# One Strassen level for the widening MLP product, its weight sums on VectorE

## The chip, the cores and the metric

The kernel runs on one core of one Trainium2 chip. The metric is the device time of one launch in microseconds (us). TensorE (PE in the profile) multiplies; VectorE (DVE), ScalarE (ACT) and GpSimd (POOL) do the rest; SyncE (SP) issues most DMAs. L203 and the like are lines of the kernel before; lines of the changed kernel are higher by 46 in its helpers.

## The reference

One step of a two-layer decoder trunk for 512 prompt rows and 64 sample rows, which share the weights; the kernel keeps them as 576 columns (NT) of one activation matrix with 1024 rows (D_MODEL), in float32. Per layer: a norm, the input product, attention and pooling branches, gates, the product with w_o, and then the part that is changed:

```python
h2 = rmsnorm(x, norm2)
x = x + jnp.square(jax.nn.relu(h2 @ w_up)) @ w_down
```

`w_up` is 1024 x 4096 (the widening product), `w_down` 4096 x 1024 (the narrowing one). Outputs are the two activations after a last norm, and the updated caches and pool states.

## The kernel before

**Two-part operands.** Every product runs in float32r. A weight tile (128 x 1024, 512 KB) is fetched into `raw`, copied by ACT to a high part `wh` (`wsplit`), and DVE subtracts to get a low part `wl` (`settle`). Activations are split likewise (`split`). A product of one 128-row weight block with an activation block is three passes: high by high, high by low, low by high. Each pass covers 576 columns as two matmuls of 256 and 320 columns (`HALF`), so that they fall into two PSUM banks; `gemm8` (through `gemm`, L228) runs eight blocks of 128 rows, 48 matmuls, into one PSUM buffer `mm`, of which there are two.

**The MLP.** Layers run one after the other, and in each the product with w_o ends in eight tiles `xs[f]` (the residual) and eight split tiles `h2`, already scaled by the gains of the second norm; the norm's own factor `rb` is applied later. The widening product has 32 tiles of 128 rows, the narrowing product eight. They alternate in four chunks: eight widening tiles, then the eight narrowing tiles of the chunk before, each of which adds the contribution of eight widening tiles to `xs[f]`. For a widening tile, `relu2` takes the PSUM buffer by one DVE instruction (`z`, ReLU and factor), squares it on ACT (`zz`) and splits it. For a narrowing tile DVE adds the buffer to `xs[f]` (`xr<-xr,mm`). In layer 0 the last chunk also squares and splits for the next layer (`hn`); in layer 1 `last` runs it in column ranges of 320 and 256 and `finish` does the last norm.

**What sets the order.** The program is written out by hand: engines run their own instructions in the order in which the Python code emits them. `wnext()` hands out the next weight tile and, while doing so, emits the fetch of tiles up to five places ahead and the split of tiles up to three places ahead; `wh` and `wl` have three buffers each. `side(...)` and `tick(...)` place side work by a planned clock. `move` emits a one-element DVE copy (`beat`) that paces cache copies on POOL's DMA queue. All helpers record their DVE, ACT and POOL instructions under one line (L203), so the rows below are told apart by the names of the tiles.

Of the kernel before, what the change touches and what calls it, by code (L numbers as in the profile page):

```python
# [7 lines left out]
F32 = mybir.dt.float32  # L8
# [23 lines left out]
NCONST = _n  # L32

UNITS = ("d", "a", "b", "e", "c")


@with_exitstack
def hybrid_decoder_kernel(ctx: ExitStack, tc: tile.TileContext, a, o):
# [36 lines left out]
    def g2(l, k):  # L75
        return gains[:, 16 + 8 * l + k:16 + 8 * l + k + 1]
# [10 lines left out]
    for l in range(L):  # L87
        for p in range(2):
            for u, unit in enumerate(UNITS):
                if unit == "e" and p == 1:  # L90
                    continue
                seq += [(a["wq"][l, p, u, i], 1024) for i in range(2)]
        seq += [(a["wu"][l, g], 1024) for g in (3, 2, 1, 0)]
        for wg, wp_, m, lead in (("wgb", "wpb", 512, LEADB), ("wga", "wpa", 256, LEADA)):
            for f in range(8):
                seq += [(a[wg][l, i], 1024) for i in range(lead[f - 1] if f else 0, lead[f])]
                seq.append((a[wp_][l, f], m))
        seq += [(a["wo"][l, f], 1024) for f in range(8)]
        for c in range(5):
            if c < 4:  # L100
                seq += [(a["wup"][l, 8 * c + f], 1024) for f in range(8)]
            if c:
                seq += [(a["wd"][l, c - 1, f], 1024) for f in range(8)]
    raws, cut, owed, spare = [], [], [], []
    pos = [0, 0, 0]

    def wfetch(n):
        while pos[0] < min(n, len(seq)):
            src, w = seq[pos[0]]
            raw = wp.tile([128, 1024], F32, tag="raw", name="raw", bufs=2)  # L110
            Q.dma_start(raw[:, :w], src)
            raws.append((raw, w))
            pos[0] += 1

    def wsplit(n):
        while pos[1] < min(n, len(seq)):
            raw, w = raws[pos[1]]
            if pos[1] < len(seq) - 5:
# [5 lines left out]
            owed.append((lo[:, :w], raw[:, :w], hi[:, :w].bitcast(F32)))  # L124
            cut.append((hi, lo))
            pos[1] += 1

    def settle():
        while owed:
            V.tensor_sub(*owed.pop(0))  # L130

    def wnext():
        i = pos[2]
        pos[2] += 1
        wfetch(i + 2)
        for n in range(1, 4):
            settle()
            wsplit(i + n)
            if n < 3:
                settle()  # L140
                wfetch(i + 2 + n)
        post(1.2, settle)

        def ahead():
            settle()
            wfetch(i + 5)

        post(2.0, ahead)
        return cut[i]
# [5 lines left out]
    def side(gen, delay=0.0):  # L155
        sides.append([now[0] + delay if not isinstance(delay, tuple) else delay, gen])
# [79 lines left out]
    def gemm8(w, acts):  # L236
        return gemm([(*wcols(w, k), acts[k]) for k in range(8)])
# [118 lines left out]
    for l in range(L):  # L356
# [691 lines left out]
        h2 = []  # L1048
        sqs = tp.tile([128, NT], F32, tag="sqs", name="sqs", bufs=1)
        for f in range(8):  # L1050
            if f == 0:
                first = pair8(mixed)
            elif f == 1:
                wnext()
            ps = first.pop(0) if f < 2 else gemm8(wnext(), mixed)
            V.tensor_add(xs[f], xs[f], ps)
            t = fp.tile([128, 2, NT], F32R, tag="h2", name="h2")
            split(t, xs[f], g2(l, f))
            square(xs[f], sqs, f)
            h2.append(t)  # L1060
        side(stats(sqs, False, ("b", l)), 2.4)
# [5 lines left out]
        hn = []  # L1067

        def down(c, fts):
            for f in range(8):  # L1070
                ps = gemm8(wnext(), fts)
                V.tensor_add(xs[f], xs[f], ps)
                if c == 3:
                    square(xs[f], sqs, f)
                    t = ap.tile([128, 2, NT], F32R, tag="a", name="a")
                    split(t, xs[f], g1(l + 1, f))
                    hn.append(t)
                    Q.dma_start(x_dr[f], xs[f])
                move(xs[f][0:1, 0:1])

        def relu2(c, ps, fts):
            t = fp.tile([128, NT], F32, tag="z", name="z", bufs=3)
            V.scalar_tensor_tensor(out=t, in0=ps, scalar=0.0, in1=scale_of["b", l][1], op0=ALU.max, op1=ALU.mult)
            t2 = fp.tile([128, NT], F32, tag="zz", name="zz", bufs=3)
            S.activation(t2, t, AF.Square)
            if c % 2 == 0:
                ft = ap.tile([128, 2, NT], F32R, tag="a", name="a")
            else:
                ft = mp_.tile([128, 2, NT], F32R, tag="m", name="m")
            split(ft, t2)  # L1090
            fts.append(ft)
            move(ft[0:1, 0, 0:1].bitcast(F32))
            return
            yield

        pend = None
        for c in range(4):
            fts = []
            for f in range(8):
                if f == 2:  # L1100
                    until("R", ("b", l))
                ps = gemm8(wnext(), h2)
                side(relu2(c, ps, fts), ("R", ("b", l)))
                tick()
            if pend is not None:
                down(c - 1, pend)
            pend = fts

        def finish(t0, t1, parts, end):
            n = t1 - t0  # L1110
# [31 lines left out]
                if not end:  # L1142
                    yield 0.9

        def last(fts):
            ws = []
            for t0, t1 in ((0, 320), (320, NT)):
                n = t1 - t0
                sq = tp.tile([128, NT], F32, tag="sqs", name="sqs", bufs=1)
                for f in range(8):  # L1150
                    if t0 == 0:
                        ws.append(wnext())
                    ps = mmp.tile([128, 1024], F32, tag="mm", name="mm")
                    for k in range(8):
                        for j, (w, x) in enumerate(((0, 0), (0, 1), (1, 0))):
                            T.matmul(ps[:, 0:n], wcols(ws[f], k)[w], fts[k][:, x, t0:t1],  # L1156
                                     start=(k == 0 and j == 0), stop=(k == 7 and j == 2))
# [12 lines left out]

        if l + 1 < L:
            down(3, pend)
        else:
            spare += 8 * [lambda: fp.tile([128, 2, NT], F32R, tag="h2", name="h2")]
            spare += 2 * [lambda: ap.tile([128, 2, NT], F32R, tag="a", name="a")]
            last(pend)
        while movers:
            move(xs[7][0:1, 0:1])
        h = hn
# [127 lines left out]
```

## Time and profile before

| | us |
|---|---|
| median of 3 runs | 1770.21 (1767.9 to 1780.41) |
| the profiled execution | 1771.32 |
| its span, first to last instruction | 1769.3 |
| PE busy in the span | 1678.0 (95%) |
| DVE, ACT, POOL busy | 941.1 (53%), 553.6 (31%), 440.1 (25%) |

The profiled execution lies 1.1 us above the median of the runs and 2.0 us above its own span. Busy shares are averages over stages with different limits: in the attention stages PE waits at places, in the MLP stages it does not, and the share of DVE in the MLP is lower than over the whole span.

### The profile page before, as it was taken

The page shows a single profiled execution, that of the slowest core. Times are in us where ns is not written, and L with a number is a line of the kernel's source. Part 1 is how long each engine was busy: PE and PEld are TensorE (multiplying, and loading weights), DVE is VectorE, ACT ScalarE, POOL GpSimd, SP SyncE. Part 2 cuts the span into 40 slices and gives each one's busy share as a digit, 9 for nine tenths or more (in the row PEclk, how much of TensorE's full clock was granted, in tenths as well). Part 3 has the DMA queues.
Part 4 walks back from the last instruction along what each step waited for, and adds up shares of the span by engine and source line. Part 5 has one row for each costly group of instructions (what it writes and reads, how often), then busy time and mean ns, then how long its engine had stood idle before and what let it go on. Part 6 is the DMA issues. An engine that isn't in the chain of part 4 may idle for free. (4 is left out here: it accounts for less than half of the span.)

```text
span 1769.3 us, 30870 instructions
## 1 busy us (share of the span) xinstructions
PE 1678.0 (95%) x12992; PEld 1632.7 (92%) x12992; DVE 941.1 (53%) x1365; ACT 553.6 (31%) x882; POOL 440.1 (25%) x461
## 2 busy tenths in 40 slices
PE   8978799999999999999997897989999999999996
PEld 7978789989999999999997886888999999999996
DVE  6488679735444333343536975894454443433332
ACT  5523332223333222231334242311334331313232
POOL 2074129211111211110103712562111112121211
PEclk9979899999999999999999998999999999999998
DMA  5552654434254445443327336435243454444421
GB/s 171 170 163 66 219 158 127 135 105 155 85 186 165 171 155 178 153 170 109 130 74 229 118 116 208 136 100 163 78 157 120 169 168 166 167 166 164 165 84 54
DMA packets 140003, 255.22 MB, mean 144 GB/s; under 512 B 9660, under 2 KB 100284, under 8 KB 137034
## 3 DMA queue, kind: packets, MB, share of 16 engines
q1 hardware_dynamic: 135498, 198.46, 35.0%
q0 software_dynamic: 3648, 53.98, 8.6%
q8 instruction: 102, 1.67, 0.4%
q10 hardware_dynamic: 720, 0.82, 0.1%
q14 instruction: 35, 0.29, 0.1%
HBM read 239.40 MB, written 74.87 MB: 178 GB/s over the span
## 5 line engine op out<-in xcount | busy, mean ns | idle before, releaser
L228 PE MATMUL mm<-a,wh 128*128 128x256 f32 (+1 forms) x2304 | 413.2, 302 | 8.8 <-DVE tb L203 8.8
L203 DVE TENSOR_TENSOR wl<-raw,wh 128x1024 fp32r<-128x1024 f32 (+2 forms) x248 | 330.6, 1334 | 110.1 <-ACT wh L203 100.3
L203 ACT CAST wh<-raw 128x1024 fp32r<-128x1024 f32 (+2 forms) x248 | 241.4, 973 | 399.9 <-PE mm L228 301.4
L228 PEld LDWEIGHTS mm<-a,wh 128*128 128x128 f32 x2304 | 350.1, 192 | 16.9 <-issue 16.0
L228 PE MATMUL mm<-h,wh 128*128 128x256 f32 (+1 forms) x2048 | 354.8, 295 | 0.0
L228 PEld LDWEIGHTS mm<-h,wh 128*128 128x128 f32 x2048 | 306.2, 188 | 0.2
L203 POOL TENSOR_TENSOR prod<-kc,qb 128x1024 f32<-128x1024 f32 (+1 forms) x96 | 210.0, 2217 | 226.6 <-DMA kc<-in_c 183.8
L228 PE MATMUL mm<-a,wl 128*128 128x256 f32 (+1 forms) x1152 | 249.9, 299 | 0.0
L458 PE MATMUL mmq<-wh,a 128*128 128x256 f32 x1152 | 225.1, 295 | 3.2 <-DVE a L203 3.0
L228 PE MATMUL mm<-h,wl 128*128 128x256 f32 (+1 forms) x1024 | 218.1, 295 | 0.0
L203 POOL COPY pace<-beat 1x1 f32<-1x1 f32 x112 | 66.9, 597 | 545.1 <-DVE beat L203 545.1
L228 PE MATMUL mm<-m,wh 128*128 128x256 f32 (+1 forms) x1152 | 200.1, 295 | 0.0
L228 PEld LDWEIGHTS mm<-a,wl 128*128 128x128 f32 x1152 | 197.3, 192 | 0.0
L458 PEld LDWEIGHTS mmq<-wh,a 128*128 128x128 f32 x1152 | 187.4, 199 | 6.9 <-DVE a L203 3.8
L203 DVE TENSOR_TENSOR xr<-xr,mm 128x576 f32<-128x576 f32 (+2 forms) x88 | 61.5, 699 | 245.3 <-PE mm L228 223.1
L228 PEld LDWEIGHTS mm<-m,wh 128*128 128x128 f32 x1152 | 173.3, 187 | 0.0
L228 PEld LDWEIGHTS mm<-h,wl 128*128 128x128 f32 x1024 | 171.5, 188 | 0.0
L458 PE MATMUL mmq<-wl,a 128*128 128x256 f32 x576 | 167.4, 291 | 0.0
L203 ACT ACTIVATE zz<-z 128x576 f32<-128x576 f32 x64 | 43.9, 686 | 259.7 <-DVE z L203 259.7
L228 PE MATMUL mm<-m,wl 128*128 128x256 f32 x576 | 123.3, 295 | 0.0
L203 DVE SCALAR_TENSOR_TENSOR z<-mm,rb 128x576 f32<-128x576 f32 x64 | 48.5, 757 | 134.6 <-PE mm L228 128.1
L458 PEld LDWEIGHTS mmq<-wl,a 128*128 128x128 f32 x576 | 114.6, 199 | 0.0
(211 smaller groups left out, 1928.2 us busy)
## 6 DMA issues: line engine op xcount, KB each, us to landing
raw<-in_wup SPq DMA_DIRECT2D x64, 512.0 KB
raw<-in_wd SPq DMA_DIRECT2D x64, 512.0 KB
out_s<-in_c POOLq DMA_DIRECT2D x64, 508.0 KB, 4.0
kc<-in_c SPq DMA_DIRECT2D x40, 512.0 KB
raw<-in_wq SPq DMA_DIRECT2D x35, 512.0 KB
kc<-in_c SPq DMA_DIRECT2D x64, 256.0 KB
out_s<-in_c POOLq DMA_DIRECT2D x32, 504.0 KB, 4.7
raw<-in_wgb SPq DMA_DIRECT2D x16, 512.0 KB
```

The lines of the kernel that those rows point to most:

```text
L203: return op(*args, **kw)
L228: T.matmul(ps[:, c0:c0 + t1 - t0], w, act[:, x, t0:t1], start=(i == 0 and j == 0), stop=(i == n - 1 and j == 2))
L458: T.matmul(psm[:, j], x, ww, start=(k == 0 and i == 0 and j % 2 == 0), stop=(k == 7 and i == 2 and j % 2 == 1), skip_group_check=True)
```

## The change

Two widening tiles (a pair, `up(j)`, j from 0 to 15 in each layer) are computed together as a 2 x 2 block product in the Winograd form of Strassen's scheme: the weights of the pair are cut in two output tiles by two halves of the 1024 rows, the activations in two halves of the rows by two halves of 288 columns (`NH`). Seven products of four blocks and 288 columns (`product`, 12 matmuls each) take the place of eight. They are B11, B21, T2, T1, T3, B22, T4 in this order (for j = 0, T1 stands before B21), called by the names of their activation operands.

- **Activations**: `blocks(f)`, behind each w_o tile, forms B11 and T1 = B12 - B11 for f < 4, and for f > 3 B21, B22, T3, T2, T4, all split into high and low parts.
- **Weights**: a pair has four entries in the sequence: the tile `r0`; `ws` (two sums); `r0` overwritten by two more sums; the second half of `r1`. `Two.first` and `Two.second` are four DVE instructions of 512 columns. 3.5 tiles are split per pair, where there were two.
- **PSUM**: B11, T2, T3 and T4 accumulate in the first bank of an `mm` buffer (A), B21 goes to its second bank (B), T1 and B22 accumulate in a bank of their own (C, tile `pc`). Between the products the partial sums are read out: ACT copies A after B11 (e1), A after T2 (u2), C after T1 (e5) into the tile `e`, and A after T4 into `z`; DVE adds e1 + B, e5 + A after T3, u2 + C after B22 into two tiles `z`.
- **Order**: `MLP` alternates one pair with half a chunk of the narrowing product: up 0, up 1, up 2, down 0, up 3, down 1, ... up 15, down 13, down 14, down 15. A chunk is now four widening tiles, so a narrowing tile is 24 matmuls and there are twice as many, each with its DVE addition; a `down` is four of them, from two weight tiles.

```diff
+    def first(self, eng):
+        eng.tensor_add(self.s[:, h1], self.r1[:, h0], self.r1[:, h1])
+        eng.tensor_sub(self.s[:, h0], self.s[:, h1], self.r0[:, h0])
+    def second(self, eng):
+        eng.tensor_sub(self.r0[:, h0], self.r1[:, h0], self.r0[:, h0])
+        eng.tensor_sub(self.r0[:, h1], self.r0[:, h1], self.s[:, h0])
...
+        def product(dst, w, half, name, start, stop):
+            for k in range(4):
+                c = slice(512 * half + 128 * k, 512 * half + 128 * k + 128)
+                for j, (m, x) in enumerate(((0, 0), (0, 1), (1, 0))):
+                    T.matmul(dst, w[m][:, c], ops[name][k][:, x], start=(start and k == 0 and j == 0),
+                             stop=(stop and k == 3 and j == 2), skip_group_check=True)
+                tick(0.4)
...
+        def up(j):
+            ps = mmp.tile([128, 1024], F32, tag="mm", name="mm")
+            pc = opp.tile([128, 512], F32, tag="o", name="pc")
+            A, B, C_ = ps[:, 0:NH], ps[:, 512:512 + NH], pc[:, 0:NH]
...
+            w = wnext()
+            product(A, w, 0, "B11", True, False)
+            S.copy(e1, A)
...
+            product(B, w, 1, "B21", True, True)
+            z_open()
+            V.tensor_add(z[0][:, :NH], e1, B)
+            if j:
+                w1 = wnext()
+            product(A, w1, 0, "T2", False, False)
+            S.copy(u2, A)
+            if j:
+                product(C_, w1, 1, "T1", True, False)
+                S.copy(e5, C_)
+            w = wnext()
+            product(A, w, 0, "T3", False, False)
+            z_open()
+            V.tensor_add(z[1][:, NH:], e5, A)
+            product(C_, w, 1, "B22", False, True)
+            V.tensor_add(z[0][:, NH:], u2, C_)
+            side(relu2(z[0]), ("R", ("b", l)))
+            w = wnext()
+            product(A, w, 0, "T4", False, True)
+            S.copy(z[1][:, :NH], A)
+            side(relu2(z[1]), ("R", ("b", l)))
```

Where instructions move, the order of the two programs shows it. First PE, at the start of a widening tile before: one wait for the free buffer, and then 48 matmuls.

```order
L228 MATMUL mm<-h_4833,wl 128x320
L228 MATMUL mm<-h_4450,wh 128x256 [waits DVE_49]
L228 MATMUL mm<-h_4450,wh 128x320
L228 MATMUL mm<-h_4450,wh 128x256
L228 MATMUL mm<-h_4450,wh 128x320
L228 MATMUL mm<-h_4450,wl 128x256
L228 MATMUL mm<-h_4450,wl 128x320
```

PE in a pair of the changed kernel, from the first matmul of B21 to the first of T2 (`h_4663` to `h_4884` are the four operands B21, `h_4670` the first of T2).

```order
L1173 MATMUL mm<-h_4663,wh 128x288 [waits Activation_49]
L1173 MATMUL mm<-h_4663,wh 128x288
L1173 MATMUL mm<-h_4663,wl 128x288
L1173 MATMUL mm<-h_4735,wh 128x288 x2
L1173 MATMUL mm<-h_4735,wl 128x288
L1173 MATMUL mm<-h_4812,wh 128x288 x2
L1173 MATMUL mm<-h_4812,wl 128x288
L1173 MATMUL mm<-h_4884,wh 128x288 x2
L1173 MATMUL mm<-h_4884,wl 128x288
L1173 MATMUL mm<-h_4670,wh 128x288 [waits DVE_49]
```

Both products now begin with a wait: B21 for an instruction of ACT (by its count on the semaphore, the copy e1), T2 for one of DVE (by its count, the addition e1 + B). Further on in the pair, T3 and B22 wait for ACT (u2, e5) and T4 for DVE (e5 + A).

Second DVE, at the first narrowing tiles of a chunk before.

```order
L203 TENSOR_TENSOR m<-zz,m 128x576
L203 COPY beat<-m 1x1
L203 TENSOR_TENSOR wl<-raw,wh 128x1024
L203 TENSOR_TENSOR xr<-xr,mm 128x576
L203 COPY beat<-xr 1x1
```

DVE in the changed kernel, from the addition u2 + C behind B22 to the addition of the first narrowing tile of the `down` that follows (`rawu` holds r0 and r1, `rb` the norm's factor).

```order
L249 TENSOR_TENSOR z<-e,pc 128x288
L249 SCALAR_TENSOR_TENSOR z<-z,rb 128x576
L249 TENSOR_TENSOR wl<-raw,wh 128x1024
L249 SCALAR_TENSOR_TENSOR z<-z,rb 128x576
L249 TENSOR_TENSOR ws<-rawu 128x512
L249 TENSOR_TENSOR ws<-ws,rawu 128x512
L249 TENSOR_TENSOR wl<-rawu,wh 128x1024
L249 TENSOR_TENSOR rawu<-rawu 128x512
L249 TENSOR_TENSOR rawu<-rawu,ws 128x512
L249 TENSOR_TENSOR m<-z,m 128x576
L249 COPY beat<-m 1x1
L249 TENSOR_TENSOR xr<-xr,mm 128x576
```

The four sums and the split of the next pair's r0 stand between the pair's own last additions and the narrowing tile's addition, which the third narrowing tile waits for before it may write that buffer.

## Rows read from the trace of the kernel before

**Rows 1.** The page, parts 1 and 2: busy time by engine; granted clock in 40 slices.

```profile
PE 1678.0 (95%) x12992; PEld 1632.7 (92%) x12992; DVE 941.1 (53%) x1365; ACT 553.6 (31%) x882; POOL 440.1 (25%) x461
PEclk9979899999999999999999998999999999999998
```

**Rows 2.** Busy time by stretch: the MLP of layers 0 and 1.

```profile
core 0: us, PE busy (x) PEld busy (x) DVE busy (x) ACT busy (x) POOL busy (x), PEclk, DMA share, GB/s
475.00:860.00 385.00, 385.00 (x2900) 384.81 (x2899) 153.66 (x219) 109.13 (x134) 63.60 (x115) 1.00 0.45 157
1350.00:1735.00 385.00, 385.00 (x2892) 384.85 (x2890) 150.59 (x224) 112.69 (x145) 64.32 (x118) 1.00 0.44 152
```

**Rows 3.** Timeline (start, us, engine, instruction), DVE: two narrowing tiles in a row.

```profile
854.86 0.76 DVE L203 TENSOR_TENSOR xr<-xr,mm 128x576 f32<-128x576 f32 x1 [1.59 <-PE mm L228]
861.26 0.76 DVE L203 TENSOR_TENSOR xr<-xr,mm 128x576 f32<-128x576 f32 x1 [1.59 <-PE mm L228]
```

**Rows 4.** Timeline, PE: matmuls of 256 columns alone, three between the rows' starts.

```profile
905.68 0.40 PE L458 MATMUL mmq<-wh,a 128*128 128x256 f32 x2
906.04 0.40 PE L458 MATMUL mmq<-wh,a 128*128 128x256 f32 x2
```

**Rows 5.** Timeline: the end of a tile and its reader; PE released by DVE.

```profile
484.60 0.42 PE L228 MATMUL mm<-h,wl 128*128 128x256 f32 x2
484.86 0.69 PE L228 MATMUL mm<-h,wh 128*128 128x256 f32 x4
485.06 0.76 DVE L203 SCALAR_TENSOR_TENSOR z<-mm,rb 128x576 f32<-128x576 f32 x1 [1.22 <-PE mm L228]
...
1174.77 0.74 DVE L203 TENSOR_TENSOR tb<-mm,rb 128x576 f32<-128x576 f32 x1
1175.66 0.79 PE L228 MATMUL mm<-a,wh 128*128 128x256 f32 x4 [2.46 <-DVE tb L203]
```

**Rows 6.** Timeline, DVE: instructions of 512, 368 and 256 columns.

```profile
331.99 0.68 DVE L203 TENSOR_TENSOR wl<-raw,wh 128x512 fp32r<-128x512 f32 x1
332.59 0.53 DVE L203 TENSOR_TENSOR SC<-SC,const 128x368 f32<-128x368 f32 x1
333.15 0.80 DVE L203 TENSOR_REDUCE dsm<-SC 128x16 f32<-128x368 f32 x1
...
1737.94 0.42 DVE L203 TENSOR_TENSOR xr<-xr,mm 128x256 f32<-128x256 f32 x1 [1.43 <-PE mm L1156]
```

**Rows 7.** Groups of DVE's instructions in 475 to 860 us (count, busy us, mean ns).

```profile
L203 DVE TENSOR_TENSOR wl<-raw,wh 128x1024 fp32r<-128x1024 f32 x60 | 74.0, 1234 | 5.0 <-issue 0.3
L203 DVE COPY beat<-xr 1x1 f32<-1x1 f32 x24 | 3.1, 140 | 1.5
```

**Rows 8.** Timeline, ACT: casts of 1024 and 576 columns, copies from PSUM of 512 and 256.

```profile
486.57 0.67 ACT L203 CAST a<-zz 128x576 fp32r<-128x576 f32 x1
487.15 1.04 ACT L203 CAST wh<-raw 128x1024 fp32r<-128x1024 f32 x1
...
478.95 0.58 ACT L203 COPY rb<-rps 128x512 f32<-128x512 f32 x1 [0.85 <-PE rps L308]
1756.21 0.37 ACT L203 COPY rb<-fb 128x256 f32<-128x256 f32 x1 [2.25 <-PE fb L1128]
```

**Rows 9.** Busy time by stretch (columns as in Rows 2): attention of both layers.

```profile
120.00:130.00 10.00, 8.04 (x61) 7.25 (x59) 10.00 (x10) 4.53 (x9) 6.76 (x4) 0.83 0.17 61
160.00:170.00 10.00, 9.78 (x61) 9.80 (x62) 7.32 (x10) 3.25 (x3) 0.00 (x0) 0.70 0.24 86
980.00:990.00 10.00, 8.31 (x67) 7.71 (x65) 8.04 (x8) 1.53 (x2) 7.67 (x4) 1.00 0.81 260
990.00:1000.00 10.00, 8.41 (x73) 7.76 (x74) 9.97 (x16) 5.24 (x10) 3.90 (x2) 1.00 0.01 2
```

**Rows 10.** Groups by form over the span: the 512-column weight split, beside POOL's products.

```profile
L203 DVE TENSOR_TENSOR wl<-raw,wh 128x512 fp32r<-128x512 f32 x18 | 33.0, 1834 | 4.1 <-ACT wh L203 4.1
```

More of the change, by code (lines that the diff above doesn't have):

```diff
@@ L34, with __init__ @@
 UNITS = ("d", "a", "b", "e", "c")
+MLP = []
+for _j in range(16):
+    MLP.append(("up", _j))
+    if _j > 1:
+        MLP.append(("down", _j - 2))
+MLP += [("down", 14), ("down", 15)]
+NH = NT // 2
+class Two:
+    def __init__(self, *src):
+        self.src = src
+    def first(self, eng):
+        h0, h1 = slice(0, 512), slice(512, 1024)
+        eng.tensor_add(self.s[:, h1], self.r1[:, h0], self.r1[:, h1])
+        eng.tensor_sub(self.s[:, h0], self.s[:, h1], self.r0[:, h0])
+    def second(self, eng):
+        h0, h1 = slice(0, 512), slice(512, 1024)
+        eng.tensor_sub(self.r0[:, h0], self.r1[:, h0], self.r0[:, h0])
+        eng.tensor_sub(self.r0[:, h1], self.r0[:, h1], self.s[:, h0])
 @with_exitstack
@@ L98, in hybrid_decoder_kernel @@
         seq += [(a["wo"][l, f], 1024) for f in range(8)]
[L99 to L103, printed above, removed]
+        for kind, j in MLP:
+            if kind == "up":
+                two = Two(a["wup"][l, 2 * j], a["wup"][l, 2 * j + 1])
+                seq += [(two, i) for i in range(4)]
+            else:
+                seq += [(a["wd"][l, j // 2, 2 * (j % 2) + n], 1024) for n in range(2)]
     raws, cut, owed, spare = [], [], [], []
@@ L109, in wfetch @@
             src, w = seq[pos[0]]
-            raw = wp.tile([128, 1024], F32, tag="raw", name="raw", bufs=2)
-            Q.dma_start(raw[:, :w], src)
-            raws.append((raw, w))
+            if not isinstance(src, Two):
+                raw = wp.tile([128, 1024], F32, tag="raw", name="raw", bufs=2)
+                Q.dma_start(raw[:, :w], src)
+                raws.append((raw, w))
+            elif w == 0:
+                src.r0, src.r1 = (fp.tile([128, 1024], F32, tag="rawu", name="rawu", bufs=4) for _ in range(2))
+                Q.dma_start(src.r1, src.src[1])
+                Q.dma_start(src.r0, src.src[0])
+                raws.append(None)
+            else:
+                raws.append(None)
             pos[0] += 1
@@ L116, in wsplit @@
         while pos[1] < min(n, len(seq)):
-            raw, w = raws[pos[1]]
-            if pos[1] < len(seq) - 5:
+            two, w = seq[pos[1]]
+            then = None
+            if not isinstance(two, Two):
+                raw, w = raws[pos[1]]
+            elif w == 0:
+                raw, w = two.r0, 1024
+                two.s = fp.tile([128, 1024], F32, tag="ws", name="ws", bufs=2)
+                two.first(V)
+                then = two.second
+            else:
+                raw, w = ((two.s, 1024), (two.r0, 1024), (two.r1[:, 512:1024], 512))[w - 1]
+            if pos[1] < len(seq) - 1:
                 hi = wp.tile([128, 1024], F32R, tag="wh", name="wh", bufs=3)
@@ L123, in wsplit @@
             S.copy(hi[:, :w], raw[:, :w])
-            owed.append((lo[:, :w], raw[:, :w], hi[:, :w].bitcast(F32)))
+            owed.append((then, lo[:, :w], raw[:, :w], hi[:, :w].bitcast(F32)))
             cut.append((hi, lo))
@@ L129, in settle @@
         while owed:
-            V.tensor_sub(*owed.pop(0))
+            then, *args = owed.pop(0)
+            V.tensor_sub(*args)
+            if then is not None:
+                then(V)
     def wnext():
@@ L1056, in hybrid_decoder_kernel @@
             V.tensor_add(xs[f], xs[f], ps)
-            t = fp.tile([128, 2, NT], F32R, tag="h2", name="h2")
-            split(t, xs[f], g2(l, f))
+            blocks(f)
             square(xs[f], sqs, f)
-            h2.append(t)
-        side(stats(sqs, False, ("b", l)), 2.4)
+        side(stats(sqs, False, ("b", l)), 5.0)
         mark("ffn", l, lat=8.0)
@@ L1066, in hybrid_decoder_kernel @@
             sqs = tp.tile([128, NT], F32, tag="sqs", name="sqs", bufs=1)
[L1067 to L1078, printed above, removed]
-                move(xs[f][0:1, 0:1])
@@ L1081, in relu2 @@
[L1081 to L1090, printed above, removed]
+        hn, fts = [], []
@@ new lines, in down_out, with wd @@
+        def down_out(c, f, ps):
+            V.tensor_add(xs[f], xs[f], ps)
+            if c == 7:
+                square(xs[f], sqs, f)
+                t = ap.tile([128, 2, NT], F32R, tag="a", name="a")
+                split(t, xs[f], g1(l + 1, f))
+                hn.append(t)
+                Q.dma_start(x_dr[f], xs[f])
+            if f % 2:
+                move(xs[f][0:1, 0:1])
+        def wd(w, i, k):
+            return tuple(v[:, 256 * k + 128 * i:256 * k + 128 * i + 128] for v in w)
@@ new lines, in down @@
+        def down(j):
+            c = j // 2
+            for n in range(2):
+                w = wnext()
+                for i in range(2):
+                    while len(fts) < 4 * c + 4:
+                        tick(0.3)
+                    ps = gemm([(*wd(w, i, k), fts[4 * c + k]) for k in range(4)])
+                    down_out(c, 4 * (j % 2) + 2 * n + i, ps)
+        def product(dst, w, half, name, start, stop):
[5 more added lines that the diff above has]
+                tick(0.4)
@@ L1091, in relu2 @@
+        def relu2(z):
+            V.scalar_tensor_tensor(out=z, in0=z, scalar=0.0, in1=scale_of["b", l][1], op0=ALU.max, op1=ALU.mult)
+            yield 0.8
+            S.activation(z, z, AF.Square)
+            ft = mp_.tile([128, 2, NT], F32R, tag="m", name="m")
+            S.copy(ft[:, 0], z)
+            yield 1.5
+            V.tensor_sub(ft[:, 1], z, ft[:, 0].bitcast(F32))
             fts.append(ft)
             move(ft[0:1, 0, 0:1].bitcast(F32))
-            return
-            yield
@@ L1143, in finish, with last @@
                     yield 0.9
-        def last(fts):
+        def last():
             ws = []
@@ L1169, in last @@
                 tick(0.3)
[L1171 to L1176, printed above, removed]
+        for kind, j in MLP:
+            if kind == "up":
+                if j == 1:
+                    until("R", ("b", l))
+                up(j)
+            elif j < 14 or l + 1 < L:
+                down(j)
+            elif j == 14:
+                spare += 2 * [lambda: ap.tile([128, 2, NT], F32R, tag="a", name="a")]
+                last()
         while movers:
```

66 lines of the change are left out of this document (48 added, 18 removed).

## Prediction, made before the changed kernel ran

> **What bounds the kernel now.** I read the busy shares first, then the stretches of the MLP, then single instructions. PE is busy 95% of the span [rows 1], and in the two MLP stretches 385.00 of 385 us at the full clock, with DVE at 40% and ACT at 28% [rows 2]: whatever takes matmuls away there shortens the kernel one for one, until another engine makes PE wait. A tile of 48 matmuls takes 6.40 us [rows 3], so a matmul takes 0.133 us on average. One of 256 columns takes 0.36 / 3 = 0.12 us [rows 4], so one of 320 takes 0.147, and one of 288, midway, 0.133.
>
> **What is removed.** A pair of widening tiles has 96 matmuls now and 84 afterwards: 12 x 0.133 = 1.60 us, times 32 pairs = 51.2 us. PE was the bound, so this comes off whole. The narrowing product keeps its columns; its tiles are halved and doubled in number.
>
> **What is added inside a pair.** The order gives PE a wait at the head of five of the seven products, each for a read of the product just before or two before. Prices: a result can be read 0.20 us after PE's slot has ended (the next tile's first matmul starts at 484.86, the reader at 485.06), PE starts again 0.15 us after its releaser (1175.51 to 1175.66), and its first four matmuls then take 0.79 us where they take 0.69 in a stream [rows 5]. A copy of 288 columns by ACT from PSUM is taken as 0.40 us, between 0.37 (256) and 0.58 (512) [rows 8]; an addition on DVE as 0.45, between 0.42 (256) and 0.53 (368) [rows 6].
> - B21 waits for the copy e1 of the product directly before it: nothing lies between. 0.20 + 0.40 + 0.15 + 0.10 = 0.85 us.
> - T2 waits for the addition e1 + B, directly behind B21: 0.20 + 0.45 + 0.15 + 0.10 = 0.90 us.
> - T3 and B22 wait for u2 and e5, with a whole product (1.60 us) in between: hidden.
> - T4 waits for e5 + A on DVE, which stands behind the split of the narrowing product's weight tile, whose cast stands behind e5 on ACT. From the end of T1: 0.20 + 0.40 + 1.04 + 0.05 + 1.23 + 0.37 + 0.15 [rows 5, 7, 8] = 3.44 us against two products of 1.60; with the slower start 0.35 us.
>
> Together 2.1 us per pair, 67 us in all. This alone is more than the matmuls give back. Bounds: 1.65 us per pair, if the slow start is nothing and T4 waits 0.1, and 2.6, if each of the three handovers costs 0.15 more.
>
> **What is added in front of a narrowing tile.** There are two `mm` buffers, so the third narrowing tile of a `down` starts when DVE has added the first one to `xs`. Between e5 + A and that addition stand the rows shown in the order: 0.45 + 0.76 + 1.23 + 0.76 + 2 x 0.68 + 1.23 + 2 x 0.68 + 0.76 + 0.14 + 0.76 = 8.8 us. Eight of them can start 0.08 us before their predecessor ends and three, which need its result, 0.03 after it [rows 6]: -0.55. The second `z` step waits 0.8 us for ACT, which has a cast, a square, a cast and a copy to do first (1.04 + 0.67 + 0.67 + 0.40 [rows 8]). That is 9.05 us from a point 0.25 us ahead of T4; T4 and two tiles are 1.6 + 3.2 + 3.2 = 8.0 us. With restart and slow start PE stands 1.0 us. It occurs where a next pair's sums follow, 13 times per layer: 26 us. No row shows a float32 sum of 512 columns; 0.68 us is the subtraction of that size, which also reads two tiles and writes one. Its other end is 1.83 us, the mean of that form where POOL multiplies beside it [rows 10]; I take the quiet end, since POOL in the MLP only paces copies. If the sums overlapped fully the 1.0 us would be 0; with no overlap at all between DVE's instructions it would be 1.9.
>
> **What is added at the start of the MLP, per layer.** `blocks` puts seven DVE and five ACT instructions behind each of the last four w_o tiles, in turns. When tile 6 ends, DVE has 3.5 us of sums and splits to finish; then comes one chain, each step waiting for the one before: for tile 6 addition, scaling, cast, two steps of DVE, two casts, the square and a weight cast, 0.76 + 0.7 + 0.7 + 1.25 + 0.7 + 0.4 + 0.65 + 0.95 = 6.1 us by the rows used above, that weight's split (1.3), and the same for tile 7 with the copy e1 at its end (6.4). PE has tile 7, B11 and T1 for it, 9.6 us, and so stands 7.7. Then T2 waits 2.0 us (the cast and split of a half tile are in front of e1 + B), T3 0.85 (in pair 0 no product lies between), T4 1.4 (the norm's statistics, four sums and a split in front); in pairs 1 and 2 the e1 copies stand behind the squares and casts of the pair before (2.2 and 2.3), T2 0.9 each, T4 1.55 and 0.35, since pair 1 has sums and no narrowing tiles to give DVE time. 20.2 us, of which 6.3 is counted above: 13.9 per layer, 28 in all, between 14 and 40.
>
> **The clock.** A long wait is followed by a stretch at 1.2 GHz: 0.70 mean over the 10 us behind an idle PE in attention, 3.0 us lost [rows 9]. I add that once per layer for the wait of pair 0: 6 us. Short waits did not lower it at 980 to 1000 us, with PE busy 83 and 84% and the clock at 1.00, a share that the steady pairs stay above (24.0 of 27.1 us); at 120 to 130, after a wait of some 2 us, the mean was 0.83 [rows 9]. The Trainium skill ("TensorE: Matmul & The Clock Gate", section "A second HAM failure mode: psum-queue depth-cycling") tells of a kernel whose PE idles briefly between groups as it cycles through PSUM, and whose clock swings between its two levels for it; by that rule this change would be slower still, and it is the fourth rival.
>
> **What costs nothing.** ACT's extra casts (1.5 tiles per pair) and copies leave it near 40% busy under PE. The weight bytes are the same and fetched a whole pair ahead. The doubled additions to `xs` (0.76 us each) lie beside the tiles of 3.2 us; without that cover they would cost 24 us per layer. The last chunk of layer 1 is halved but has the same columns, its reads (0.42 us) fit into 1.44 us per tile.
>
> **Sum.** -51 + 67 + 26 + 28 + 6 = +76 us. On the profiled execution's 1771.3 us that gives 1847; the median of the runs lies 1.1 us lower: 1846 us.
>
> **Rivals.**
> - *Not slower.* If B21's and T2's waits are met before PE comes to them (the wait belongs to an older instruction, or PE's queue runs ahead of it), 1.75 us per pair go, 56 us, and at the start the waits of T2 and for e1, 12.4 us of 20.2 per layer: -51 + 11 + 26 + 15 + 3 = +4, 1775 us. It decides at the first matmul of B21 and T2: below 0.1 us of idle there. For it: the order names an engine, and only the count says which instruction. Against: the counts are those of the reads, and a read cannot end before its product has.
> - *All is hidden.* The wait of the narrowing tile and the start vanish too, and 51 us come off: 1720 us. For it: DVE and ACT have room on average. Against: DVE's rows add up to 9 us in 8.
> - *DVE is the bound.* If its sums take 1.0 us instead of 0.68, the third narrowing tile waits 1.3 us longer in 28 places: +36, 1882 us. For it: DVE's mean is above the quiet figure wherever POOL works. Against: POOL has no multiplications in the MLP.
> - *The clock gives way.* One such stretch as at 120 to 130 per pair, 1.7 us in 28 places: +48, 1894 us. For it: two waits of 0.9 us lie only 1.6 us apart. Against: the rows at 980 to 1000.
>
> **Chances.** Forecast 0.66, not slower 0.07, all hidden 0.04, DVE 0.12, clock 0.11. The range is 1792 (1.65 us per pair, no wait of the narrowing tile, starts 14, clock 6: -51 + 53 + 14 + 6 = +22) to 1888 (narrowing tiles 1.9 us, starts 40, clock 12: -51 + 67 + 50 + 40 + 12 = +118), both on the median; the DVE case ends inside. It leaves out the first two rivals and most of the clock's. A measurement of this kernel can tell about 1%, 18 us, from no change: faster by more 0.04, within it 0.07, slower 0.89.
>
> **What would show it.** PE busy well under full in the MLP; idle of 0.8 to 0.9 us ahead of B21, released by ACT, and ahead of T2, released by DVE, in every pair; about 1 us ahead of every third narrowing tile, released by `xr`; one wait of some 5 us in pair 0; a pair with its `down` taking 27.1 us where four tiles took 25.6. I am wrong if those idle times are missing, if matmuls of 288 columns do not take 0.133 us, or if the granted clock in the steady pairs falls below 1.00.

## The result, and the profile after

The changed kernel takes 1869.88 us (median of 4 runs, 1867.15 to 1873.11); the kernel before took 1774.5 us in the same series. The ratio is 1.054, with a 95% interval of 1.049 to 1.059: slower, where 1846 us had been forecast. The profiled execution took 1873.11 us, its span is 1871.3 us, 102 us more than before; the sum of the prediction was +76.

Parts 1 and 2 of the page (beside [rows 1]): 384 matmuls fewer, PE's share down from 95 to 90%, DVE's up to 63%.

```profile
PE 1686.0 (90%) x12608; PEld 1611.8 (86%) x12608; DVE 1183.9 (63%) x1765; ACT 668.4 (36%) x1106; POOL 433.6 (23%) x461
PEclk9989899999799999999998998999997999999998
```

Busy time by stretch (columns as in [rows 2]). Where PE had no idle time in 385 us it now has 38.7, and the mean clock is 0.96. The last three stretches tell the two apart: in the steady pairs (640 to 700 us) the clock is 1.00 and PE idle, at the start of the MLP it is 0.50, the lower of the two levels (1.2 GHz).

```profile
475.00:860.00 385.00, 346.31 (x2426) 333.70 (x2427) 233.47 (x367) 144.02 (x212) 58.73 (x114) 0.96 0.44 146
640.00:700.00 60.00, 56.02 (x409) 54.27 (x408) 36.99 (x56) 23.74 (x35) 8.40 (x16) 1.00 0.45 149
480.00:490.00 10.00, 4.84 (x20) 4.14 (x19) 5.59 (x9) 5.12 (x8) 0.00 (x0) 0.50 0.22 59
490.00:500.00 10.00, 9.51 (x42) 9.13 (x43) 6.22 (x17) 1.55 (x3) 0.00 (x0) 0.50 0.52 177
```

Timeline of PE, one steady pair with its `down`; the bracket gives the idle time before a row and its releaser. From above: T4 of the pair before, the first and the third narrowing tile, then B11, B21 and T2.

```profile
696.58 0.53 PE L1173 MATMUL mm<-h,wh 128*128 128x288 f32 x2
...
698.28 0.69 PE L274 MATMUL mm<-m,wh 128*128 128x256 f32 x4
...
705.73 0.80 PE L274 MATMUL mm<-m,wh 128*128 128x256 f32 x4 [0.89 <-DVE xr L249]
...
712.23 0.42 PE L1173 MATMUL mm<-h,wh 128*128 128x288 f32 x2
...
714.46 0.53 PE L1173 MATMUL mm<-h,wh 128*128 128x288 f32 x2 [0.49 <-ACT e L249]
...
716.92 0.53 PE L1173 MATMUL mm<-h,wh 128*128 128x288 f32 x2 [0.62 <-DVE z L249]
```

A product without a wait takes 1.60 us from start to start. B11 to B21 takes 2.23, B21 to T2 2.46 and, with T2's own slow start, T2 to T1 1.71; with 0.14 around T4 a pair loses 1.74 us. From the first to the third narrowing tile 7.45 us pass for 6.40 us of work, and the next two tiles take 0.10 more. So a pair with its `down` takes 26.87 us (B11 at 712.23, the next at 739.09): 24.0 + 1.74 + 1.15.

DVE in front of the third narrowing tile: from e5 + A, 0.5 us ahead of T4, over the sums to the addition that PE waits for. Each sum of 512 columns takes 0.68 to 0.69 us, as assumed.

```profile
696.08 0.45 DVE L249 TENSOR_TENSOR z<-e,mm 128x288 f32<-128x288 f32 x1
...
700.41 0.68 DVE L249 TENSOR_TENSOR ws<-rawu 128x512 f32<-128x512 f32 x1
701.13 0.69 DVE L249 TENSOR_TENSOR ws<-ws,rawu 128x512 f32<-128x512 f32 x1
...
704.94 0.73 DVE L249 TENSOR_TENSOR xr<-xr,mm 128x576 f32<-128x576 f32 x1
```

The start of the MLP of layer 0, PE's waits in pair 0 (T1 twice, B21, T2) and at B21 of pair 1. From the first product (471.04) to the first narrowing tile 66.0 us pass, in layer 1 63.6; at the full clock and without a wait it would be three pairs and the norm's statistics, 33.5 + 2.5 us (the statistics as in the kernel before).

```profile
476.00 0.53 PE L1173 MATMUL pc<-h,wh 128*128 128x288 f32 x2 [3.22 <-ACT wh L249]
477.71 0.61 PE L1173 MATMUL pc<-h,wl 128*128 128x288 f32 x1 [1.18 <-DVE wl L249]
484.09 0.85 PE L1173 MATMUL mm<-h,wh 128*128 128x288 f32 x2 [3.60 <-ACT e L249]
488.89 0.85 PE L1173 MATMUL mm<-h,wh 128*128 128x288 f32 x2 [1.56 <-DVE z L249]
...
507.90 0.54 PE L1173 MATMUL mm<-h,wh 128*128 128x288 f32 x2 [2.49 <-ACT e L249]
```

### The profile page after: what moved, and what is told of

Same layout as the page of the kernel before. It is cut to its first block, busy times and chain, and to the rows that moved or that the text cites. A ratio compares the mean times of both kernels' runs of the same rounds, so it can differ in the third digit from the quotient of the medians.

```text
span 1871.3 us, 30691 instructions
## 1 busy us (share of the span) xinstructions
PE 1686.0 (90%) x12608; PEld 1611.8 (86%) x12608; DVE 1183.9 (63%) x1765; ACT 668.4 (36%) x1106; POOL 433.6 (23%) x461
## 5 line engine op out<-in xcount | busy, mean ns | idle before, releaser
L274 PE MATMUL mm<-m,wh 128*128 128x256 f32 (+1 forms) x2304 | 403.1, 296 | 24.3 <-DVE xr L249 24.2
L274 PEld LDWEIGHTS mm<-m,wh 128*128 128x128 f32 x2304 | 345.0, 188 | 30.7 <-DVE xr L249 29.4
L1173 PE MATMUL mm<-h,wh 128*128 128x288 f32 x1280 | 279.9, 311 | 53.8 <-ACT e L249 29.8
L274 PE MATMUL mm<-a,wh 128*128 128x256 f32 (+1 forms) x1280 | 237.1, 309 | 10.6 <-DVE tb L249 6.2
L274 PE MATMUL mm<-m,wl 128*128 128x256 f32 (+1 forms) x1152 | 246.6, 295 | 0.0
L274 PEld LDWEIGHTS mm<-a,wh 128*128 128x128 f32 x1280 | 197.7, 196 | 18.5 <-issue 18.0
L1173 PE MATMUL mm<-h,wl 128*128 128x288 f32 x640 | 194.8, 304 | 0.0
L274 PEld LDWEIGHTS mm<-m,wl 128*128 128x128 f32 x1152 | 193.2, 188 | 0.0
L274 PE MATMUL mm<-a,wl 128*128 128x256 f32 (+1 forms) x640 | 140.2, 302 | 0.0
L1173 PE MATMUL pc<-h,wh 128*128 128x288 f32 x512 | 107.4, 302 | 6.4 <-ACT wh L249 6.4
```

Source lines behind the costliest of these rows:

```text
L274: T.matmul(ps[:, c0:c0 + t1 - t0], w, act[:, x, t0:t1], start=(i == 0 and j == 0), stop=(i == n - 1 and j == 2))
L1173: T.matmul(dst, w[m][:, c], ops[name][k][:, x], start=(start and k == 0 and j == 0), stop=(stop and k == 3 and j == 2), skip_group_check=True)
```

## The experiments

Ratios are against the kernel before, run on the same chip. Each edit starts from the changed kernel unless another is named. "Start" is the stretch from the first product to the first narrowing tile, layer 0 and layer 1; a "step" is a steady pair with its `down`. Starts are read from one execution each, and the same program does not always give the same one: e1, e5 and e6 have the same instructions on PE, DVE and ACT up to the first narrowing tile, and their starts were 48.7, 48.7 and 48.6 us in layer 0, but 52.9, 49.9 and 49.9 in layer 1, with mean clocks of 0.87, 0.90 and 0.90. A difference of up to 3 us in one start alone therefore shows no effect of an edit.

**e1_own_bank: B21 gets its own PSUM tile.**

```diff
-            A, B, C_ = ps[:, 0:NH], ps[:, 512:512 + NH], pc[:, 0:NH]
+            pb = pdp.tile([128, 512], F32, tag="d", name="pb")
+            A, B, C_ = ps[:, 0:NH], pb[:, 0:NH], pc[:, 0:NH]
```

> The product B21 gets a PSUM tile of its own (pd) and no longer shares the mm tile with A. Theory (B21 waits for the copy e1, and T2 for the sum e1 + B, only because A and B are two halves of one tile): both idle times go, 0.64 and 0.87 us of each pair's 12.9 us, 48 us over 32 pairs, and a pair with its down takes about 25.4 us instead of 26.87; with a little more at the start of the MLP 1815 to 1825 us. Rival 1 (the handover is a real one: PE waits before B21 for something else that ends at the same time): 26.87 us stays, 1870 us. Rival 2 (the wait moves on to T4, whose sum e5 + A stands on DVE behind the split of a weight tile): T4 waits 0.5 us or more and 16 us or more come back, 1835 us and over.

1793.66 us, ratio 1.015 (1.012 to 1.017), below the 1815 to 1825 us expected: of the 95 us lost, 76 came back by the medians and 70 by the ratios, with two lines changed. The timeline of PE shows B11, B21 (`pb`), T2 and the next pair's B11 with no bracket.

```profile
606.77 0.43 PE L1173 MATMUL mm<-h,wh 128*128 128x288 f32 x2
...
608.35 0.43 PE L1173 MATMUL pb<-h,wh 128*128 128x288 f32 x2
...
609.93 0.43 PE L1173 MATMUL mm<-h,wh 128*128 128x288 f32 x2
...
632.01 0.43 PE L1173 MATMUL mm<-h,wh 128*128 128x288 f32 x2
```

The step is 25.24 us, 1.64 less (1.5 expected), 43 us in 26 steps. Both waits were therefore waits for the tile, not for the data: B21 does not read what e1 copies, and B lay in a bank of its own, the buffer's second, before the edit too. The start shrank more than expected, from 66.0 and 63.6 to 48.7 and 52.9 us, 28 us in both layers, because the waits fell from 16.9 to some 9 us per layer and part of the time at half clock went with them (mean clock 0.97 and 0.87, against 0.77 and 0.81). The other 7.5 us of the span lie ahead of the two MLP parts, where the edit has nothing.

**e2_late_sums: the sums behind the first two narrowing tiles.** `first` is called ahead of the cast of `ws`, one weight tile later; `heads` holds the first pair of each layer.

```diff
             elif w == 0:
...
-                two.first(V)
-                then = two.second
+                if pos[1] in heads:
+                    two.first(V)
+                    then = two.second
             else:
+                if w == 1 and pos[1] - 1 not in heads:
+                    two.first(V)
+                    then = two.second
```

> The four weight sums of every pair but the first are given to DVE behind the additions of the first two narrowing tiles of a down, not ahead of them; nothing else moves. Theory (the third narrowing tile waits because 2.7 us of sums stand in front of the first one's addition): DVE's rows are then 6.4 us against 8.0 us of PE, the 0.89 us of idle with its slow start (1.15 us, 26 times) goes, 30 us: 1840 us. Rival 1 (ACT's part of the z step sets it): 0.3 us or more stay, 1850 us and over. Rival 2 (the wait moves to the next pair's B11, whose buffer the third narrowing tile's addition must free): idle before B11, 1870 us.

1865.01 us, ratio 1.055 (1.053 to 1.057): 5 us, not 30. The third narrowing tile waits no more, but B11 of the next pair does (timeline of PE, two successive B11):

```profile
609.13 0.50 PE L1180 MATMUL mm<-h,wh 128*128 128x288 f32 x2 [0.31 <-DVE xr L256]
...
635.40 0.50 PE L1180 MATMUL mm<-h,wh 128*128 128x288 f32 x2 [0.31 <-DVE xr L256]
```

The step is 26.27 us, so 0.60 of 1.15 us were gained and the rest became rival 2's wait. And the edit cost something that no theory had: pairs 1 and 2 have no `down` before them, the later cast of `ws` stood ahead of e1 on ACT, and B21 waited 4.99 and 4.81 us there. The start took 70.3 and 72.0 us.

**e3_spread_rows: the w_o tiles in the order 0, 4, 1, 5, 2, 6, 3, 7.**

```diff
-        seq += [(a["wo"][l, f], 1024) for f in range(8)]
+        seq += [(a["wo"][l, f], 1024) for f in ROWS]
...
-        for f in range(8):
-            if f == 0:
+        for i, f in enumerate(ROWS):
+            if i == 0:
```

> The eight w_o tiles are computed in the order 0, 4, 1, 5, 2, 6, 3, 7, so that tiles with seven DVE and five ACT instructions behind them (4 to 7) alternate with light ones. Theory (tile 7's addition stands behind work of tile 6 and the split of the weight sums, so that one chain runs through both): 3.2 + 1.2 us of waiting before and in T1 fall to under 1 us in each layer, the 3.6 us before B21 stay, and some of the time at half clock goes with it: 10 to 16 us in all, about 1857 us. Rival (the order of the weight's casts on ACT sets it, whatever the rows' order): the waits of pair 0 stay at 8 us and the time at 1870 us.

1863.81 us, ratio 1.053 (1.051 to 1.056); the start took 59.1 and 60.3 us. T1's waits fell from 4.4 to 1.4 us (0.19 and 1.19), but 0.40 us came up inside B11, and B21 waited 4.79 us in place of 3.60 (these in layer 0). The starts are 3 and 7 us shorter, which is the theory's direction, but only 1.3 us of layer 0's 7 are waits (15.6 in place of 16.9 in all); the rest goes with a mean clock of 0.88 in place of 0.77. The median, 6 us lower, is not well apart from the changed kernel's.

**e4_fill: PE busy while it waits.** Matmuls into a bank that nobody reads, ahead of T1, B21 and T2 in pair 0 and of B21 in pairs 1 and 2.

```diff
+        def fill(w, n):
+            pd = pdp.tile([128, 512], F32, tag="d", name="fill")
+            for i in range(n):
+                T.matmul(pd[:, 0:NH], w[0][:, 0:128], ops["B11"][i % 4][:, 0], start=True, stop=True)
...
+                fill(w, 24)
                 product(C_, w1, 1, "T1", True, False)
...
+            if j < 3:
+                fill(w, (24, 14, 10)[j])
             product(B, w, 1, "B21", True, True)
...
+            if j == 0:
+                fill(w, 8)
             product(A, w1, 0, "T2", False, False)
```

> PE multiplies operands that are already there into a bank that nobody reads, just ahead of the products it waits for in pairs 0 to 2 (24 + 24 + 8, 14 and 10 matmuls of 288 columns per layer, 0.133 us each at the full clock). They are sized to fit into the idle time and take no other engine's. Theory (about 11 us per layer at the start of the MLP are matmuls at half the clock behind the long waits, not waits): the granted clock stays near 1.00 between 470 and 560 us and 8 to 11 us per layer go, 1848 to 1855 us. Rival 1 (the stretch is bound by DVE and ACT alone, and PE's slower matmuls are hidden in it): under 3 us per layer, 1865 to 1870 us. Rival 2 (the fill is longer than the waits): slower than 1870 us.

1858.23 us, ratio 1.050 (1.048 to 1.052): for 160 matmuls more, 12 us less by the medians and 6 by the ratios, whose intervals overlap; the two starts of the trace are 7 us shorter. Stretches of this run, layer 0 (beside 0.50 and 0.50 above) and layer 1, and T2 of pair 0 in both layers:

```profile
480.00:490.00 10.00, 6.58 (x49) 6.09 (x48) 4.83 (x10) 5.10 (x9) 0.00 (x0) 0.97 0.30 107
490.00:500.00 10.00, 9.51 (x63) 8.97 (x63) 7.97 (x18) 4.52 (x8) 0.00 (x0) 0.86 0.37 130
...
1400.00:1410.00 10.00, 9.45 (x43) 9.08 (x44) 6.23 (x18) 2.07 (x4) 0.00 (x0) 0.54 0.57 183
```

```profile
487.47 0.53 PE L1173 MATMUL mm<-h,wh 128*128 128x288 f32 x2 [1.80 <-DVE z L249]
...
1400.06 0.53 PE L1173 MATMUL mm<-h,wh 128*128 128x288 f32 x2 [1.80 <-DVE z L249]
```

The start took 59.6 and 62.6 us: 6.4 us less in layer 0, where the mean clock was 0.97, and 0.9 in layer 1, where it was 0.92. T2 still waited 1.80 us in both, and the waits that were left add up to 8.9 us in both; the clock fell behind T2 in both too, for longer in layer 1. Why is not shown. B21 and T2 begin 13.1 and 17.8 us behind the first product, as in the changed kernel (13.1 and 17.9): what T1 gained by the clock, B21 waited out, which is rival 1 for these three products. All the 6.4 us lie behind T2. So the mechanism is the theory's and the size is not: the time stayed above the 1848 to 1855 us expected.

**e5_own_late and e6_own_late_a.** e5 joins e1 and e2, with `heads` holding pairs 0 to 2; in e6 A leaves the `mm` buffers as well.

```diff
-            ps = mmp.tile([128, 1024], F32, tag="mm", name="mm")
+            if j < 3:
+                ps = mmp.tile([128, 1024], F32, tag="mm", name="mm")
+            else:
+                ps = trp.tile([128, 512], F32, tag="tr", name="pa")
```

> B21 in its own bank as in e1_own_bank, and the sums behind the additions of the first two narrowing tiles as in e2_late_sums, but only for pairs that follow a down (pairs 0 to 2 keep their order). Theory (the sums stay in front of the addition of the second-last pair of narrowing tiles, which frees the buffer that A of the next pair takes): the third narrowing tile no longer waits (1.15 us), B11 waits 0.3 us and starts slowly, so a pair with its down takes 24.6 to 24.7 us instead of 25.24, 15 to 17 us in all: about 1778 us. Rival (the wait at B11 came from the pair waits' timing and is gone without them): 24.1 us, 1764 us.

> As e5_own_late, and from pair 3 on A has a bank of its own too (the one that the norm's statistics use earlier), so that no widening product takes an mm buffer. Theory: nothing in a pair or a down waits any more, 24.0 to 24.1 us for 180 matmuls (84 of 288 columns and 96 halves of 256 and 320); 30 us less than e1_own_bank, about 1764 us. Rival 1 (DVE's additions of T3 and T4 then become the wait, as PE comes to T4 earlier): T4 idle 0.3 us or more, 1772 us and over. Rival 2 (another turnaround at PSUM, not the mm buffers, makes B11 wait): as e5_own_late.

e5: 1778.47 us, ratio 1.004 (1.002 to 1.006). e6: 1761.55 us, ratio 0.994 (0.991 to 0.996). Both theories hold to 3 us. Two successive B11 of e5, then of e6 (timeline of PE):

```profile
585.18 0.50 PE L1179 MATMUL mm<-h,wh 128*128 128x288 f32 x2 [0.32 <-DVE xr L255]
...
609.79 0.50 PE L1179 MATMUL mm<-h,wh 128*128 128x288 f32 x2 [0.31 <-DVE xr L255]
```

```profile
576.10 0.43 PE L1179 MATMUL pa<-h,wh 128*128 128x288 f32 x2
...
600.17 0.43 PE L1179 MATMUL pa<-h,wh 128*128 128x288 f32 x2
```

The step is 24.61 and 24.07 us; in e6 PE waits for nothing between 580 and 860 us. That closes the account of the steady pairs: 26.87 = 24.07 + 1.64 for B's place, and 1.15 for the sums' place, half of which needs A's place too.

**e7_start: e6 with the order of e3, and pair 0's weights fetched and first summed earlier.**

```diff
             blocks(f)
             square(xs[f], sqs, f)
+            if i == 0:
+                up0 = next(s for s, w in seq[pos[2]:] if isinstance(s, Two))
+                ufetch(up0)
+            elif i == 4:
+                ufirst(up0)
```

> As e6_own_late_a, with the w_o tiles in the order of e3_spread_rows, and for pair 0 the two weight tiles fetched and the first two sums made some four tiles earlier. Theory (at the start PE waits for one chain on DVE and ACT behind tile 7, and what stood ahead of it were the sums and their split): the waits of T1 fall from 4.4 to under 1.5 us per layer, those of B21 and T2 together stay under 4 us, and the start is 5 to 6 us shorter per layer: 1752 to 1755 us, faster than the kernel before by about 1%. Rival (the chain behind tile 7 hides nothing, what T1 gains B21 and T2 lose): as e6_own_late_a, 1764 us.

1767.39 us (ratio 0.998, 0.996 to 0.999), no faster than e6. By the time it is the rival, by the waits it is not: those of layer 0 fell from 7.7 to 5.1 us, with T1's under 1.5 as the theory had it and B21's unchanged at 0.73, and in layer 1 from 8.1 to 6.5. The start took 46.6 and 50.9 us against 48.6 and 49.9, with a mean clock of 0.93 and 0.87 against 0.93 and 0.90: 2 us gained in one layer and 1 lost in the other, no more than the same program can differ by. Nor was tile 7's addition any sooner, so the sums were not what held it up. ACT and then DVE, in front of tile 7's addition (the w_o product ended at 474.9):

```profile
476.10 0.68 ACT L265 ACTIVATE sq<-xr 128x576 f32<-128x576 f32 x1
476.68 1.03 ACT L265 CAST wh<-ws 128x1024 fp32r<-128x1024 f32 x1
```

```profile
477.75 1.68 DVE L265 TENSOR_TENSOR wl<-ws,wh 128x1024 fp32r<-128x1024 f32 x1 [0.76 <-ACT wh L265]
479.35 0.74 DVE L265 TENSOR_TENSOR xr<-xr,mm 128x576 f32<-128x576 f32 x1
```

The addition stands behind a weight's split, the split behind its cast, the cast behind the square of the tile before.

**e8_casts_first and e9_casts_only: the casts ahead.** `wnext` for the next tile is called before a tile's addition; e9 has the rows in their old order and the first sums one tile earlier.

```diff
-            ps = first.pop(0) if i < 2 else gemm8(wnext(), mixed)
+            ps = first.pop(0) if i < 2 else gemm8(ready, mixed)
+            if i:
+                ready = wnext()
```

> As e7_start, and the cast of the weight tile that is needed three tiles later is given to ACT ahead of the work behind each w_o tile (ahead of its addition and its scaling, casts and square), no longer behind its square. Theory (what e7_start left is that on DVE the addition of a w_o tile stands behind the split of a weight, whose cast stands on ACT behind the square of the tile before, so that all eight tiles form one chain longer than PE's 6.4 us each): tile 7's addition then begins within 1 us of the tile's end and not 4.5 us after it, T1 and B21 wait under 1 us, T2 some 1 to 2 us, the stretch from the first product to the first narrowing tile takes 39 to 42 us in place of 48.6, and the time is 1745 to 1750 us. Rival (the chain is one of DVE's own instructions, the casts are met anyway): 46 us and more, 1757 to 1762 us.

> As e8_casts_first, with the w_o tiles in their old order 0 to 7. Theory of the chain: tiles 4 to 7 each need 6.1 to 6.6 us of chained work for 6.4 us of PE, so the old order with the casts ahead is only 0 to 3 us per layer slower than e8_casts_first: 1746 to 1755 us. Rival (the spread is what helps): as e6_own_late_a, 1762 us.

1759.88 us (0.994, 0.992 to 0.996) and 1760.13 us (0.993, 0.991 to 0.996). Only part of the theory came true: in e8 tile 7's addition began at 471.55, 3.0 us after the tile's end (4.5 in e7, under 1 expected), T1 and B21 waited under 1 us, but T2 2.25. The waits of the start add up to 6.0 and 5.6 us, less than in e6 (7.7 and 8.1) but in sum no less than in e7 (5.1 and 6.5), and the start still takes 48.8 and 48.3 us. In e9 T1 waits 3.55 us and T2 1.04, and the time is the same as in e8: neither theory's time came, and the order of the rows only moves a wait. What follows the wait stands in two rows of e8, T2 in pair 0 and the stretch behind it:

```profile
477.45 0.53 PE L1197 MATMUL mm<-h,wh 128*128 128x288 f32 x2 [2.25 <-ACT e L265]
```

```profile
480.00:490.00 10.00, 9.51 (x43) 8.89 (x44) 6.13 (x17) 2.25 (x5) 0.00 (x0) 0.59 0.62 229
```

PE is busy 9.51 of 10 us and does 43 matmuls, where a steady pair has some 68 in 10 us: in layer 0 the clock took what the waits had given against e6.

**e10_casts_fill: e8, with 16 unread matmuls ahead of T2 and 3 ahead of T3 in pair 0.** `fill` is that of e4 with another bank.

```diff
+            else:
+                fill(w, 16)
             product(A, w1, 0, "T2", False, False)
...
+            if j == 0:
+                fill(w1, 3)
             w = wnext()
             product(A, w, 0, "T3", False, False)
```

> As e8_casts_first, and in pair 0 PE multiplies operands that are already there into an unread bank while it waits: 16 matmuls of 288 columns ahead of T2 (2.1 us, in 2.25 us of idle) and 3 ahead of T3. Theory (e8_casts_first shortened the waits of the start from 8.3 to 6.0 us, but the 2.25 us one is still followed by 8 to 10 us at the 0.50 clock, which takes back 4 to 5 us per layer): the granted clock stays at 1.00 from the first product to the first narrowing tile, that stretch takes 43 to 45 us in place of 48.5, and the time is 1750 to 1753 us. Rival (the clock falls all the same behind the shorter waits of 0.5 to 1.2 us in pairs 0 to 2, or the slower products were hidden behind DVE): 47 us and more, 1757 to 1762 us.

1752.65 us, ratio 0.989 (0.988 to 0.991), as expected; the start takes 45.3 us in both layers, 3.5 and 3.1 less than in e8, at a clock of 1.00 from end to end. The intervals of e8 and e10 are apart. The unread matmuls are the only difference from e8, and they do not bring T2 forward (it starts 9.4 us behind the first product, 8.9 in e8), so these 7 us were the clock.

```profile
478.04 2.27 PE L1215 MATMUL fill<-h,wh 128*128 128x288 f32 x16
...
480.46 0.53 PE L1197 MATMUL mm<-h,wh 128*128 128x288 f32 x2 [0.15 <-ACT e L265]
```

```profile
470.00:480.00 10.00, 8.77 (x58) 7.66 (x58) 7.34 (x13) 5.78 (x9) 3.13 (x2) 1.00 0.05 12
480.00:490.00 10.00, 9.36 (x69) 8.44 (x68) 9.38 (x23) 5.94 (x10) 0.00 (x0) 1.00 0.52 181
```

This version is faster than the kernel before by 1.1%, some 19 us of the 51 that the scheme saves in matmuls. Of the rest, 2 x 9.3 us are still the starts (45.3 where 36.0 would be free of waits).

## Why the prediction was right, and where its sizes were off

The forecast case happened, and each of its five steps is in the trace; the sum was 26 us short (102 us by the spans of the profiled executions, which the table adds up; 95 by the medians).

| term of the sum | forecast, us | measured, us |
|---|---|---|
| 12 matmuls fewer per pair | -51 | -51 (a product of 12 takes 1.60) |
| waits inside the pairs | +67 (2.1 each) | +56 (1.74 each) |
| third narrowing tile | +26 (1.0 each) | +30 (1.15 each) |
| waits at the start | +28 | +28 |
| clock at the start (by subtraction) | +6 | +19 |
| everything else | 0 | +20 |

- **The pair.** With its slow start B21 loses 0.73 us (0.85 forecast) and T2 0.87 (0.90). T4 loses 0.14 and not 0.35: e5 + A ended 0.1 us sooner than priced (696.53), and PE started 0.05 us behind it and not 0.15. That the waits are real and come from B lying in A's tile is shown by e1.
- **The narrowing tile.** From T4's start DVE needs 9.1 us to the end of the addition, against 8.1 us on PE; forecast were 8.8 and 8.0. e2, e5 and e6 show the cause, and that only half of this wait goes if the sums alone are moved.
- **The waits at the start.** The brackets add up to 16.9 us in either layer. A wait of 0.49 us there costs 0.64 and 0.1 more in the slow start that follows, so the ten together cost 19.4 us; forecast were 20.2. Less the 5.2 of three pairs this is 14.2, and 28 us for both layers. That the term came out to the microsecond is in part luck: the stand behind the last w_o tile cost 8.8 us (as 3.22, 1.18 and 3.60, not as one wait of some 5) where 7.7 were forecast, and T4 of pair 0, priced at 1.4, did not wait.
- **The clock, the step that was mis-sized.** The prediction allowed one stretch of 3 us per layer behind one wait. The start takes 24.7 and 22.3 us more than three steady pairs, of which the waits are 14.2; the rest, 10.5 and 8.1 us by subtraction, is put down to work done at 1.2 GHz: three matmuls of 288 columns take 0.72 us behind 484.97 and 0.40 in the steady pairs. The long waits come one after the other (3.2, 3.6, 1.6 and 2.5 us within 35 us); the clock was 0.50 all through 480 to 500 us and 0.72 again at 520 to 530. Some 2.5 of the 10.5 us lie ahead of T2, where e4 shows that DVE and ACT would have taken the time anyway. Keeping PE busy took 6.4 us away in layer 0 (e4), and 7 us in both layers together in e10 against e8. The size is not a fixed one: the ten waits are the same to 0.01 us in both layers, and the mean clock was 0.77 in one and 0.81 in the other.
- **Everything else.** Some 10 us lie in the last three `down` of a layer and at the end, where the prediction had no wait and PE waits for the addition to `xs` (1.13 us at 919.64 and 1.42 at 928.05 in layer 0). The last chunk of layer 1, which the prediction put at nothing, has two such waits, and PE has none in these matmuls of the kernel before:

```profile
1829.23 0.53 PE L1278 MATMUL mm<-m,wh 128*128 128x320 f32 x2 [0.91 <-DVE xr L249]
...
1843.78 0.50 PE L1278 MATMUL mm<-m,wh 128*128 128x256 f32 x2 [1.65 <-DVE xr L249]
```

  The other 10.6 us lie in front of the MLP parts, 1.8 us in layer 0 and 8.8 in layer 1. Of the 8.8, one wait is the change's, that of the norm's statistics for the sum of squares, which DVE finishes late behind the last `down` (waits of PE from 928 to 1395 us; the kernel before has no such row):

```profile
PE st L333 <- DVE sqs L249: 2.1, 1, 2.1
```

  The rest was not settled: in the variants the stretch of layer 0 took 466.5 to 474.9 us and that of layer 1 460.3 to 468.1, in no order that their edits give, where the kernel before had 469.2 and 458.6.

Of the rivals, "all is hidden" fell with the waits, "DVE is the bound" with the sums' 0.68 us, and "the clock gives way" fell in the steady pairs: three waits of 0.49, 0.62 and 0.89 us per 26.87 us leave it at 1.00 from 580 to 880 us. The Trainium skill ("TensorE: Matmul & The Clock Gate", section "A second HAM failure mode: psum-queue depth-cycling") describes a clock that swings when PE idles briefly and often between groups. The steady pairs here do not show that; at the start the clock does change between its levels, but behind single waits of 1.6 to 3.2 us, and not behind each of them (it stayed up behind the 2.49 us at 507.90). The "not slower" case did not happen, but e1 bears out its price for the waits of B21 and T2: 72 us in its sum (+76 to +4), and 70 by the ratios of e1, which removes them.

## What to carry to other kernels

Before a scheme with fewer multiplications is judged, count for each product which read of which PSUM tile stands between it and the one before: two results that share a tile make PE wait for readers of the other half, and in e1 a tile of its own in a free bank took these waits away. When a wait on an in-order engine is moved, look for the next user of the same buffer, since half of it may come back there; and a start-up with several waits in a row has to be priced twice, once as idle time and once as the slower clock behind it, which also means that shortening such waits may show no gain until the clock stays up.

## What the runs showed of the hardware

DVE's sums have two durations, as the bounds of the prediction had them. In the steady pairs all are 0.68 to 0.69 us; but one per layer, at the last w_o tiles, takes 1.79. Timeline of the changed kernel, POOL and then DVE:

```profile
465.00 1.98 POOL L249 TENSOR_TENSOR sqs<-sqs,sq 128x576 f32<-128x576 f32 x1 [6.26 <-ACT sq L249]
```

```profile
465.01 0.69 DVE L249 TENSOR_TENSOR ws<-rawu 128x512 f32<-128x512 f32 x1
465.73 1.79 DVE L249 TENSOR_TENSOR ws<-ws,rawu 128x512 f32<-128x512 f32 x1
```

The slow one lies beside an addition of POOL, as does the split of 1.68 us at 477.75 in e7_start above (1.20 to 1.23 in the steady pairs). The Trainium skill ("GPSIMD Engine Reference", section "1. Specifications") says that POOL shares its way into SBUF with DVE, and that instructions with two inputs in SBUF feel it. The trace agrees for this one, but the sum before it also overlaps POOL and took 0.69 us. POOL's times in the profile are rough, so whether that sum really ran beside POOL's is not shown.
